# Turning the softmax weights of a first attention by VectorE and DMA instead of TensorE

## The chip, the core and the metric

The kernel runs on one core of a Trainium2 chip. The core has five engines with queues of their own: TensorE (PE, with PEld for its weight loads) does matrix products, VectorE (DVE) and ScalarE (ACT) do elementwise work, GpSimd (POOL) does next to nothing here, and SyncE (SP) issues nearly all DMAs. Each engine works off its instructions in the order in which the program was written, and waits where an instruction needs what another engine has not yet made. The metric is the device time in microseconds of one execution, the median of the runs shown.

## The reference

A decoder trunk of two layers on 256 tokens of width 2048, all in float32. Layer one uses the first attention, "mixer A"; layer two uses a second kind of attention; both have a squared-ReLU MLP and a gated embedding. The change lies in mixer A. For each of 8 heads there are three groups of keys, with dilations 1, 4 and 16:

```
for g, (window, dil) in enumerate(((128, 1), (512, 4), (2048, 16))):
    s   = q[g] . k[g] over the keys t, t - dil, t - 2 dil, ...   (window // dil + 1 of them)
    lse = logsumexp(s);  out_g = exp(s - lse) . v[g]
o = sum over g of softmax over g of (lse) * out_g
h = h + o @ w_out
```

The three softmaxes and the softmax over their `lse` are one softmax over all keys of the three groups together, and the kernel computes it so.

## The kernel before, in words

**Layout.** Activations lie feature-major: 128 features on the partitions, 256 tokens along the row. Each float32 weight chunk of 128 x 1024 (512 KB) is split into a high part `whi` (fp32r, ScalarE, L213) and a low part `wlo` (VectorE, L221), and each product is done as a sum over the parts. In mixer A the tokens stand in another order: first those with t mod 4 equal to 0 or 1, then the others. With dilations 4 and 16 a query then meets only keys of its own half, so the two halves `j` = 0, 1 of 128 queries need all 256 keys in the first group (the "far" products) and 128 keys in each of the other two (the "near" ones). So a head has 2 halves x (256 + 128 + 128) = 2 x 512 scores per query partition: the tile `p`, 128 x 2 x 512.

**The order of work.** `Program` holds a list of steps. Most are chunks: a weight chunk and a function that issues its matmuls. `run` does the following for every chunk, by step number: it issues loads of later weight chunks on SP (up to 7 ahead, 4 raw buffers), then the high-part copies (4 ahead) and the low-part subtractions (3 ahead), then `advance`, which takes every running generator to its next `yield`, and then the chunk's matmuls. An operation given by `prog.op` is begun between two chunks, and its first part, up to its first `yield`, is issued there. So a `yield` in a helper means "one chunk later", and the order of instructions on every engine follows from this list alone.

**Mixer A.** `v_unit` computes values (8 chunks each); for each head h six columns (`single`, i = 0 to 5; three q and three k, two chunks each) are computed, so that a head has 12 chunks, here numbered 0 to 11. The attention of head h - 1 runs among the columns of head h:

- after chunk 2, `a_scores(h - 1)`: 6 products of q and k (L827), then in the next three steps the masked maximum (VectorE, L834), the exponential (ScalarE, L838) and the scaling by 1/sum (VectorE, L841 and L843). The tile `p` then has queries on the partitions.
- after chunk 6, `a_transpose(h - 1)`: eight products with the identity (L852, 128x128 each) turn `p`, so that keys are on the partitions; a step later ScalarE copies the result out of PSUM (L858 the high part of the first group's blocks into `pt`, L859 the other groups' into `pl`), and another step later VectorE makes the low part (L861).
- after chunk 9, `a_pv(h - 1)`: the products with the values (L872 for the first group in three parts, L878 for the near groups in plain float32), then ScalarE and VectorE split the result into `oT` (L883, L885).

The attention of heads 6 and 7 ends later: head 6's `a_pv` and all that remains of head 7's come with `v_unit(5)` and the output projection. `twos` names chunks in which the products are issued in pairs, first two with the high part, then two with the low part; among others those which follow an inserted attention step. PSUM is used in two rings: `mm` (four banks) and `at` (two pairs of banks).

Of the kernel before, what the change touches and what calls it, by code (L numbers as in the profile page):

```python
# [10 lines left out]
F32 = mybir.dt.float32  # L11
F32R = mybir.dt.float32r
# [3 lines left out]
P = 128  # L16
D = 2048
T = 256
# [6 lines left out]
HA = 8  # L25
# [8 lines left out]
UNIT_AHEAD = (0, 1, 2, 4, 5)  # L34
# [7 lines left out]
def f32(ap):  # L42
    return ap.bitcast(F32)


def halved(ap):


    return ap.rearrange("p (h a s) -> p a h s", h=2, s=2)


def plain(ap):

    return ap.rearrange("p (a h s) -> p a h s", h=2, s=2)
# [90 lines left out]
def kernel(ctx: ExitStack, tc: tile.TileContext, a: dict, out: bass.AP):  # L145
    nc = tc.nc
    ctx.enter_context(tc.manual_schedule())
    prog = Program()
# [4 lines left out]
    tmp = ctx.enter_context(tc.tile_pool(name="tmp", bufs=2))  # L153
    xap = ctx.enter_context(tc.tile_pool(name="xa", bufs=KT))
    wpool = ctx.enter_context(tc.tile_pool(name="w", bufs=4))
    pspool = ctx.enter_context(tc.tile_pool(name="ps", bufs=1, space=bass.MemoryType.PSUM))

    cur = {}
# [9 lines left out]

    def bank():
        return pspool.tile([P, 512], F32, tag="mm", name="mm", bufs=4)  # L170

    def banks2():
        return pspool.tile([P, 2, 512], F32, tag="at", name="at", bufs=2)
# [20 lines left out]
    def load_x(j, order="xTA"):  # L194
        nc.sync.dma_start(xp[j], a[order][:, j * 2 * T:(j + 1) * 2 * T])
# [201 lines left out]
    def single(src, acts, done, mid=(), ring=bank, twos=()):  # L397

        st = []
        for c in range(2):  # L400
            def step(hi, lo, c=c):
                if c == 0:
                    st.append(ring())
                tiles = []
                for i in range(8):
                    k = 8 * c + i
                    tiles.append((st[0], i * P, have(acts, k), k == 0, k == KT - 1))
                mm_tiles(hi, lo, tiles, 2 if c in twos else 1)
                return [done(st[0])] if c else []
            prog.chunk(src(c), step)  # L410
            if c == 0:
                for fn in mid:
                    prog.op(fn)
# [361 lines left out]
    def square_pair(j):  # L775

        pa = cur["A"]
        if j == 0:
            cur["sum2"] = pa.tile([P, 2, 2 * T], F32, name="p", tag="p")[:, 0]
        total = cur["sum2"]  # L780
        s = f32(pa.tile([P, 2 * T], F32R, tag="oT", name="oT", bufs=HA)) if j else total
        nc.scalar.activation(s, xp[j], AF.Square)
        yield
        if j:
            nc.vector.tensor_add(total, total, s)
        if j == KT // 2 - 1:
            n_a0.acc = stat.tile([P, T], F32, tag="acc", name="acc")
            nc.vector.tensor_add(n_a0.acc, total[:, :T], total[:, T:])
            n_a0.done = KT

    qk, va, ready = {}, {}, {}
    oT = [None] * HA

    def qk_done(h, i, ps):
        if i == 0:
            qk[h] = cur["A"].tile([P, 6 * T], F32, tag="qk", name="qk", bufs=2)
            ready[h] = 0

        def mark():
            ready[h] += 1  # L800
        yield from to_head(ps, n_a0, qk[h][:, i * T:(i + 1) * T], True, mark)
# [15 lines left out]
    sm = {}  # L817

    def a_scores(h):

        prog.until(lambda: ready.get(h) == 6)
        sb = banks2()
        for j in range(2):
            own = slice(j * P, (j + 1) * P)
            for g in (1, 2, 0):
                q, k = qk[h][:, g * T:(g + 1) * T], qk[h][:, (3 + g) * T:(4 + g) * T]
                nc.tensor.matmul(sb[:, j, T + (g - 1) * P:T + g * P] if g else sb[:, j, :T], q[:, own],  # L827
                                 k[:, own] if g else k, start=True, stop=True)
        yield
        pa = cur["A"]  # L830
        p = pa.tile([P, 2, 2 * T], F32, tag="p", name="p")
        s4 = pa.tile([P, 4], F32, tag="s4", name="s4", bufs=2)
        for j in range(2):
            nc.vector.tensor_tensor_reduce(out=p[:, j], in0=sb[:, j], in1=cur["mA"][:, j], scale=-SCALE, scalar=3e38,  # L834
                                           op0=ALU.add, op1=ALU.min, accum_out=s4[:, j:j + 1])
        yield
        for j in range(2):
            nc.scalar.activation(p[:, j], p[:, j], AF.Exp, bias=s4[:, j:j + 1], scale=-1.0,  # L838
                                 accum_out=s4[:, 2 + j:3 + j])
        yield  # L840
        nc.vector.reciprocal(s4[:, 2:4], s4[:, 2:4])  # L841
        for j in range(2):
            nc.vector.tensor_scalar_mul(p[:, j], p[:, j], s4[:, 2 + j:3 + j])  # L843
        sm[h] = p

    def a_transpose(h):
        prog.until(lambda: h in sm)
        p = sm.pop(h)
        tr = banks2()
        for i in range(4):  # L850
            for j in range(2):
                nc.tensor.transpose(tr[:, i // 2, (i % 2 * 2 + j) * P:(i % 2 * 2 + j + 1) * P],  # L852
                                    p[:, j, i * P:(i + 1) * P], ident)
        yield
        pt = cur["A"].tile([P, 2, 2, T], F32R, tag="pt", name="pt", bufs=2)
        pl = cur["A"].tile([P, 2 * T], F32, tag="pl", name="pl", bufs=2)
        early = tr[:, 0].rearrange("p (b t) -> p b t", b=2)
        nc.scalar.copy(pt[:, :, 0, :], early)  # L858
        nc.scalar.copy(pl, tr[:, 1])  # L859
        yield  # L860
        nc.vector.tensor_sub(pt[:, :, 1, :], early, f32(pt[:, :, 0, :]))  # L861
        sm[h, "T"] = pt, pl

    def a_pv(h, wide=False):
        u0, u1 = h // 4 * 3, h // 4 * 3 + 1 + h % 4 // 2
        prog.until(lambda: (h, "T") in sm and ready.get(("v", u0)) == ready.get(("v", u1)) == 2)
        pt, pl = sm.pop((h, "T"))
        pv = (banks2()[:, 0, :] if wide else bank())[:, :T]
        c = slice(h % 4 * P, (h % 4 + 1) * P)
        def far(j):  # L870
            for vp, pp in ((0, 0), (0, 1), (1, 0)):
                nc.tensor.matmul(pv, va[u0][:, j, vp, c], pt[:, j, pp, :], start=j == vp == pp == 0,  # L872
                                 stop=j == vp == 1)
        far(0)
        for g in range(2):
            n = slice((h % 2 * 2 + g) * P, (h % 2 * 2 + g + 1) * P)
            for j in range(2):
                nc.tensor.matmul(pv[:, j * P:(j + 1) * P], va[u1][:, j, n], pl[:, g * T + j * P:g * T + (j + 1) * P],  # L878
                                 start=False, stop=False)
        far(1)  # L880
        yield
        o = cur["A"].tile([P, 2 * T], F32R, tag="oT", name="oT", bufs=HA)
        nc.scalar.copy(plain(o[:, :T]), halved(pv))  # L883
        yield
        nc.vector.tensor_sub(plain(o[:, T:]), halved(pv), plain(f32(o[:, :T])))  # L885
        oT[h] = o

    def v_unit(u, hooks=None, ring=bank, first=False):
        token_major(lambda c: a["w_v"][u * 8 + c], x_a0, lambda j, ps: v_done(u, j, ps), hooks, ring, first=first)
# [5 lines left out]
    for h in range(HA):  # L895
        for i in range(6):
            single(lambda c, h=h, i=i: a["w_qk"][(h * 6 + i) * 2 + c], x_a0,
                   lambda ps, h=h, i=i: qk_done(h, i, ps), mid=
                   [lambda h=h: a_scores(h - 1)] if h and i == 1 else
                   [lambda h=h: a_transpose(h - 1)] if h and i == 3 else  # L900
                   [lambda i=i: square_pair(2 * i)] if not h and i < 4 else (),
                   twos=(0,) if i == 0 and h in UNIT_AHEAD or i == 5 and 0 < h < HA - 1 else
                   (1,) if h and i == 1 else ())
            if not h and i < 4:
                prog.op(lambda i=i: square_pair(2 * i + 1))
            if not h and i == 3:
                prog.op(lambda: n_a0.factor(True))
            if 0 < h < HA - 1 and i == 4:
                prog.op(lambda h=h: a_pv(h - 1))
            if h in (2, 3) and i < 4:  # L910
                prog.op(lambda j=4 * h - 8 + i: load_x(j, order="xT"))
        u = (1, 2, None, 3, 4, None, None, 5)[h]
        if h == HA - 1:
            v_unit(5, {2: [lambda: a_scores(HA - 1)], 6: [lambda: a_transpose(HA - 1)],
                       7: []})
        elif u:
            v_unit(u)
# [427 lines left out]
    for h in range(HB):  # L1345
        mid = [lambda h=h: b_pv(h - 4)] if h >= 4 else []
        if h >= 3:
            mid.append(lambda h=h: b_transpose(h - 3))
        single(lambda c, h=h: a["w_q"][2 * h + c], x_a1, lambda ps, h=h: q_done(h, ps), mid,
               twos=(0, 1))  # L1350
# [127 lines left out]
```

## Time and profile before

| | |
|---|---|
| median of 3 runs | 2501.91 us (2501.83 to 2502.07) |
| profiled execution, its own time | 2502.39 us |
| its span, first to last instruction | 2500.6 us |
| mean granted TensorE clock | 0.999 |
| TensorE busy | 2489.7 us, 13405 matmuls |
| VectorE busy | 1655.1 us |
| ScalarE busy | 1346.8 us |
| moved by DMA | 468.47 MB, mean 187 GB/s |
| products with the identity in mixer A (L852) | 64, first at 105.5 us, last at 432.6 us |

How to read the views that follow. A table of groups has a line of the code, the engine, the operation, the tile written and those read (`at<-ident,p`: written to a tile named `at`, read from `ident` and `p`), shapes and a count. A row in order of time has the start in us, the length in us, engine, line, operation, names, shapes, and how many equal ones are merged; in brackets stands how long the engine was idle before it and what ended that. Records of matmuls overlap, because the array is pipelined and the recorded ends are modelled: what a matmul costs TensorE is the distance from its start to the next start. A row of landings has the number of DMAs, KB each, and the median time from issue to landing.

### The profile page before, as it was taken

To read this page: it belongs to the slowest core of one execution; us is meant where nothing else is said; L and a number is where in the kernel's file an instruction comes from. 1 tells how busy PE (TensorE), PEld (TensorE's weight loads), DVE (VectorE), ACT (ScalarE), POOL (GpSimd) and SP (SyncE) were. 2 spreads that over 40 slices of the span, in tenths; PEclk is the share of its full clock that TensorE was granted. 3 is DMA by queue.
4 is the path that set the end of the run, shared out by engine and by line. 5 is a ranking of instruction groups with operands and counts; after the bars stand their busy time and mean duration, and the time that the engine had idled before them with its cause. 6 is when DMAs were issued, how large, how long until landed. Compare 5 with 4: busy or idle time off the path is not lost.

```text
span 2500.6 us, 35900 instructions
## 1 busy us (share of the span) xinstructions
PE 2489.7 (100%) x13405; PEld 2144.8 (86%) x13405; DVE 1655.1 (66%) x2804; ACT 1346.8 (54%) x2162; POOL 10.4 (0%) x24
## 2 busy tenths in 40 slices
PE   9999999999999999999999999999999999999998
PEld 8888888888888888888888889988888888888887
DVE  7766676865465565566787989876546556556676
ACT  6444444554454453555664788755545445445455
POOL 0000000000000000000000000000000000000000
PEclk9999999999999999999999999999999999999999
DMA  8565555555656556656565744455555665665553
GB/s 274 176 199 190 175 169 181 180 190 190 192 193 193 189 191 194 192 189 187 187 196 188 245 160 124 146 191 188 193 193 191 191 192 192 193 191 190 185 187 130
DMA packets 131071, 468.47 MB, mean 187 GB/s; under 512 B 14736, under 2 KB 15696, under 8 KB 130896
## 3 DMA queue, kind: packets, MB, share of 16 engines
q1 hardware_dynamic: 129792, 464.31, 57.7%
q8 instruction: 105, 1.72, 0.3%
q0 software_dynamic: 528, 1.07, 0.1%
q10 hardware_dynamic: 576, 0.79, 0.1%
q14 instruction: 70, 0.57, 0.1%
HBM read 464.02 MB, written 2.10 MB: 186 GB/s over the span
## 4 chain that ended last, share of the span: by engine, by line
PE 97%; DMA 1%; DVE 1%; ACT 1%; issue 0%; SPq 0%; ACTq 0%; DVEq 0%
PE mm L352 22%; PE mm L442 18%; PE at L352 17%; PE at L442 15%; PE mm L354 11%; PE at L354 8%; DMA raw<-in_w_kv 1%; PE at L827 1%; PE at L1313 0%; DVE wlo L221 0%; PE mm L1337 0%; PE at L852 0%; PE mm L584 0%; PE mm L586 0%; PE mm L585 0%
## 5 line engine op out<-in xcount | busy, mean ns | idle before, releaser
L221 DVE TENSOR_TENSOR wlo<-raw,whi 128x1024 fp32r<-128x1024 f32 (+1 forms) x875 | 1065.6, 1219 | 632.4 <-PE at L442 131.8
L213 ACT CAST whi<-raw 128x1024 fp32r<-128x1024 f32 (+1 forms) x875 | 919.5, 1052 | 879.2 <-PE mm L442 200.0
L352 PE MATMUL mm<-xa,whi 128*128 128x512 f32 x2208 | 756.2, 395 | 0.0
L354 PE MATMUL mm<-xa,wlo 128*128 128x256 f32 x2208 | 575.2, 278 | 0.0
L352 PE MATMUL at<-xa,whi 128*128 128x512 f32 x1632 | 568.3, 394 | 0.0
L352 PEld LDWEIGHTS mm<-xa,whi 128*128 128x128 f32 x2208 | 399.2, 188 | 75.8 <-issue 0.4
L354 PE MATMUL at<-xa,wlo 128*128 128x256 f32 x1632 | 452.7, 277 | 0.0
L354 PEld LDWEIGHTS mm<-xa,wlo 128*128 128x128 f32 x2208 | 414.8, 188 | 20.4
L352 PEld LDWEIGHTS at<-xa,whi 128*128 128x128 f32 x1632 | 306.0, 187 | 70.4
L442 PE MATMUL at<-whi,h 128*128 128x512 f32 x1024 | 315.6, 389 | 0.0
L442 PE MATMUL mm<-whi,h 128*128 128x512 f32 x1024 | 315.5, 389 | 0.0
L354 PEld LDWEIGHTS at<-xa,wlo 128*128 128x128 f32 x1632 | 306.6, 188 | 0.1
L442 PEld LDWEIGHTS at<-whi,h 128*128 128x128 f32 x1024 | 191.9, 188 | 39.7
L442 PEld LDWEIGHTS mm<-whi,h 128*128 128x128 f32 x1024 | 191.5, 188 | 39.5
L442 PE MATMUL mm<-wlo,h 128*128 128x512 f32 x512 | 199.2, 389 | 0.0
L442 PE MATMUL at<-wlo,h 128*128 128x512 f32 x512 | 199.2, 389 | 0.0
L442 PEld LDWEIGHTS mm<-wlo,h 128*128 128x128 f32 x512 | 96.1, 188 | 20.0
L442 PEld LDWEIGHTS at<-wlo,h 128*128 128x128 f32 x512 | 96.1, 188 | 19.9
L360 DVE TENSOR_TENSOR et<-mm,es 128x256 f32<-128x256 f32 x137 | 55.9, 422 | 75.8 <-ACT es L358 73.9
L442 PE MATMUL mm<-whi,xa 128*128 128x512 f32 x320 | 98.9, 390 | 0.0
L358 ACT COPY es<-mm 128x256 f32<-128x256 f32 x137 | 48.4, 372 | 62.8 <-PE mm L354 59.9
L442 PEld LDWEIGHTS mm<-whi,xa 128*128 128x128 f32 x320 | 59.6, 188 | 12.3
(326 smaller groups left out, 2138.3 us busy)
## 6 DMA issues: line engine op xcount, KB each, us to landing
raw<-in_w SPq DMA_DIRECT2D x512, 512.0 KB, 3.5
raw<-in_w_qk SPq DMA_DIRECT2D x96, 512.0 KB, 3.6
raw<-in_w_gate SPq DMA_DIRECT2D x64, 512.0 KB, 4.0
raw<-in_w_kv SPq DMA_DIRECT2D x48, 512.0 KB, 4.2
raw<-in_w_v SPq DMA_DIRECT2D x47, 512.0 KB, 3.6
raw<-in_w_q SPq DMA_DIRECT2D x32, 512.0 KB, 4.5
raw<-in_w_oB SPq DMA_DIRECT2D x32, 512.0 KB, 3.5
raw<-in_w_oA SPq DMA_DIRECT2D x16, 512.0 KB, 3.5
```

The lines of the kernel that those rows point to most:

```text
L213: nc.scalar.copy(hi[:, c], t[:, c])
L221: nc.vector.tensor_sub(lo[:, c], t[:, c], f32(hi)[:, c])
L352: nc.tensor.matmul(ps, hi[:, col:col + P], rhs, start=first, stop=False)
L354: nc.tensor.matmul(ps[:, :T], lo[:, col:col + P], rhs[:, :T], start=False, stop=last)
L358: nc.scalar.copy(s, ps[:, :T])
L360: nc.vector.tensor_add(t, ps[:, T:], s)
L442: nc.tensor.matmul(st[j], *parts[j][i], start=k == i == 0, stop=k == kt - 1 and i == 2)
L827: nc.tensor.matmul(sb[:, j, T + (g - 1) * P:T + g * P] if g else sb[:, j, :T], q[:, own], k[:, own] if g else k, start=True, stop=True)
```

## The change

For heads 0 to 6 `a_transpose` is no longer called. Instead `a_scores` goes on into a new helper, `a_turn`, in the step of the scaling:

- step 5: VectorE's block transpose turns each 32x32 block of `p` (128 x 1024) in place of the block and writes it to a tile `z`, in an order in which the four blocks that belong to one group of 32 key partitions lie together (256 elements);
- step 6: SP stores `z` to a scratch tensor `dA` in DRAM (512 KB);
- step 7: SP loads it back in four DMAs of 32 partitions each to a tile `w`, so that the four partition groups of `dA` become four pieces of one row; a run in DRAM has 256 elements, 1 KB;
- step 9: ScalarE copies the first group's blocks to the high part of `pt`, putting pieces in order (two copies of 128 x 256);
- step 10: VectorE subtracts to make the low part (two of 128 x 256). The near groups' blocks stay in `w`; the products read them there, as four runs of 32 elements, 256 elements apart.

`a_pv(h - 1)` for heads 0 to 5 moves from after chunk 9 to after chunk 10 (the middle of column 5), and `twos` for column 5 moves from its first chunk to its second. Head 7 keeps `a_transpose`; its `pt` now takes a buffer of the ring `qk`, and its `pl` that of `z`. In the pool of mixer A two `pt` and two `pl` buffers (12 KB of a partition) are replaced by one `pt`, one `z` and one `w` (12 KB).

```diff
+    dpool = ctx.enter_context(tc.tile_pool(name="bounce", bufs=1, space=bass.MemoryType.DRAM))
...
+    def bounce(src, name, to):
+        m = src.shape[1] // 4
+        d = dpool.tile([P, 4 * m], F32, tag=name, name=name, bufs=2)
+        nc.sync.dma_start(d, src)
+        yield
+        d4 = d.rearrange("(a s) (b n) -> b s a n", a=4, b=4)
+        for b in range(4):
+            nc.sync.dma_start(to[32 * b:32 * b + 32], d4[b])
...
-        sm[h] = p
+        if h == HA - 1:
+            sm[h] = p
+            return
+        yield from a_turn(h, p)
+
+    def a_turn(h, p):
+        pa = cur["A"]
+        z = pa.tile([P, 4 * T], F32, tag="z", name="zA", bufs=1)
+        nc.vector.transpose(z.rearrange("p (b i j r) -> p j i b r", b=4, i=4, j=2), p.rearrange("p j (i b s) -> p j i b s", i=4, b=4))
+        yield
+        w = pa.tile([P, 4, T], F32, tag="w", name="wA", bufs=1)
+        yield from bounce(z, "dA", w)
+        yield
+        yield
+        pt = pa.tile([P, 2, 2, T], F32R, tag="pt", name="pt", bufs=1)
+        w5 = w.rearrange("p a (i j r) -> p i j a r", i=4, j=2)
+        pt6 = pt.rearrange("p i l (j a r) -> p l i j a r", j=2, a=4)
+        for i in range(2):
+            nc.scalar.copy(pt6[:, 0, i], w5[:, i])
+        yield
+        for i in range(2):
+            nc.vector.tensor_sub(pt6[:, 1, i], w5[:, i], f32(pt6[:, 0, i]))
+        sm[h, "T"] = pt, [[w5[:, 2 + g, j] for j in range(2)] for g in range(2)]
...
-        pt = cur["A"].tile([P, 2, 2, T], F32R, tag="pt", name="pt", bufs=2)
-        pl = cur["A"].tile([P, 2 * T], F32, tag="pl", name="pl", bufs=2)
+        pt = cur["A"].tile([P, 6 * T], F32R, tag="qk", name="pt", bufs=2)[:, :4 * T]
+        pt = pt.rearrange("p (i l t) -> p i l t", i=2, l=2)
+        pl = cur["A"].tile([P, 4 * T], F32, tag="z", name="zA", bufs=1)[:, :2 * T]
...
-                nc.tensor.matmul(pv[:, j * P:(j + 1) * P], va[u1][:, j, n], pl[:, g * T + j * P:g * T + (j + 1) * P],
+                nc.tensor.matmul(pv[:, j * P:(j + 1) * P], va[u1][:, j, n], pl[g][j],
                                  start=False, stop=False)
...
                    [lambda h=h: a_scores(h - 1)] if h and i == 1 else
-                   [lambda h=h: a_transpose(h - 1)] if h and i == 3 else
+                   [lambda h=h: a_pv(h - 1)] if 0 < h < HA - 1 and i == 5 else
                    [lambda i=i: square_pair(2 * i)] if not h and i < 4 else (),
-                   twos=(0,) if i == 0 and h in UNIT_AHEAD or i == 5 and 0 < h < HA - 1 else
-                   (1,) if h and i == 1 else ())
+                   twos=(0,) if i == 0 and h in UNIT_AHEAD else (1,) if h and i == 1 or 0 < h < HA - 1 and i == 5 else ())
...
-            if 0 < h < HA - 1 and i == 4:
-                prog.op(lambda h=h: a_pv(h - 1))
```

More of the change, by code (lines that the diff above doesn't have):

```diff
@@ L861, in a_transpose @@
         nc.vector.tensor_sub(pt[:, :, 1, :], early, f32(pt[:, :, 0, :]))
-        sm[h, "T"] = pt, pl
+        sm[h, "T"] = pt, [[pl[:, g * T + j * P:g * T + (j + 1) * P] for j in range(2)] for g in range(2)]
     def a_pv(h, wide=False):
```

## The prediction

> **What bounds the kernel now.** I read the page's busy times, the slices and the chain first: which engine is full, is it full everywhere, and does the end hang on it.
>
> ```profile
> span 2500.6 us, 35900 instructions
> PE 2489.7 (100%) x13405; PEld 2144.8 (86%) x13405; DVE 1655.1 (66%) x2804; ACT 1346.8 (54%) x2162; POOL 10.4 (0%) x24
> PE   9999999999999999999999999999999999999998
> PEclk9999999999999999999999999999999999999999
> PE 97%; DMA 1%; DVE 1%; ACT 1%; issue 0%; SPq 0%; ACTq 0%; DVEq 0%
> ```
>
> TensorE is busy in every slice at the full granted clock, and 97% of the chain that ended last is TensorE. So TensorE's instruction stream is the time: what leaves it is gained, as long as nothing makes it wait. Next, a table of one stretch in the first attention (head 3's columns, with head 2's attention among them; columns: TensorE, its weight loads, VectorE, ScalarE, GpSimd, clock, DMA share, GB/s) and the waits of the SP queue there.
>
> ```profile
> 147.00:185.00 38.00, 38.00 (x230) 33.63 (x229) 27.85 (x58) 17.30 (x26) 0.00 (x0) 1.00 0.60 193
> ```
> ```profile
> SPq L201 <- DVE wlo L221: 234.1, 92, 9.4
> ```
>
> In these 38 us TensorE has no idle time; VectorE has 10.15 us free, ScalarE 20.70, the DMA engines 40%. SP spent 234.1 us of the 270 us from 60 to 330 waiting for VectorE to free raw weight buffers, so it has time to issue more.
>
> Now TensorE's order of time at the products with the identity (L852), for the first, one middle and the last of the seven heads concerned (columns: start, length, instruction).
>
> ```profile
> 105.54 1.04 PE L852 MATMUL at<-ident,p 128*128 128x128 f32 x8
> 106.33 0.47 PE L352 MATMUL mm<-xa,whi 128*128 128x512 f32 x1
> 106.65 0.27 PE L354 MATMUL mm<-xa,wlo 128*128 128x256 f32 x1
> ```
> ```profile
> 163.03 0.28 PE L354 MATMUL mm<-xa,wlo 128*128 128x256 f32 x1
> ...
> 164.53 0.39 PE L352 MATMUL mm<-xa,whi 128*128 128x512 f32 x1
> 164.76 0.28 PE L354 MATMUL mm<-xa,wlo 128*128 128x256 f32 x1
> 164.88 1.04 PE L852 MATMUL at<-ident,p 128*128 128x128 f32 x8
> 165.67 0.47 PE L352 MATMUL mm<-xa,whi 128*128 128x512 f32 x1
> 165.99 0.27 PE L354 MATMUL mm<-xa,wlo 128*128 128x256 f32 x1
> ```
> ```profile
> 396.26 1.04 PE L852 MATMUL at<-ident,p 128*128 128x128 f32 x8
> 397.05 0.47 PE L352 MATMUL mm<-xa,whi 128*128 128x512 f32 x1
> 397.37 0.27 PE L354 MATMUL mm<-xa,wlo 128*128 128x256 f32 x1
> ```
>
> Records overlap, so starts count, not lengths. From the first product to the L354 that follows the next L352 it is 1.11 us in all three heads; without products, an L352 and its L354 start 164.76 − 164.53 = 0.23 apart. The eight products therefore cost 1.11 − 0.23 = 0.88 us a head. The L354 at 163.03 and the one five pairs on, at 164.76, give 0.346 us a pair and 8 × 0.346 = 2.77 us for a chunk of a `single`, the step in which everything is scheduled.
>
> **The change part by part.**
>
> *Products removed.* 7 heads (0 to 6; head 7 keeps them) × 0.88 = 6.16 us, all on TensorE, all on the path. The record lengths speak otherwise:
>
> ```profile
> L852 PE MATMUL at<-ident,p x64: 270/273/273, 105.5 to 432.6; 128*128 128x128 f32 x64
> ```
>
> Taken singly, 273 ns × 56 would be 15.3 us; the starts above exclude that, since eight records lie within 0.88 us. The Trainium skill (TensorE: Matmul & The Clock Gate, Part 4: PE-mode transpose) says a transpose took about 275 ns in one kernel's context, and 56 of those would be an estimated 15.4 us. The record length here agrees with it; the start to start time, which is what TensorE gives back, doesn't.
>
> *The products with v (`a_pv`) moved* from between columns 4 and 5 to the middle of column 5, and the pairwise order of the next chunk (`twos`) moved with it. Same instructions, same neighbours in kind; 0 us. But the softmax weights of the two near groups, the streamed operand of L878, are now read as four runs of 32 elements, 256 elements apart, instead of 128 in a row. I found no row with such a read. Before, this block was
>
> ```profile
> 174.07 0.52 PE L872 MATMUL mm<-pt,v 128*128 128x256 f32 x3
> 174.43 1.05 PE L878 MATMUL mm<-pl,v 128*128 128x128 f32 x8
> 175.24 0.60 PE L872 MATMUL mm<-pt,v 128*128 128x256 f32 x3
> 175.68 0.62 PE L352 MATMUL mm<-xa,whi 128*128 128x512 f32 x2
> ```
>
> where the eight records of L878 take 175.24 − 174.43 = 0.81 us. Bounds: 0, or the double, +0.81 × 7 = 5.7 us. A gain is excluded, since the same 128 columns stream. I take 0, since the same form in a row is the nearest row there is, and keep 5.7 for the range.
>
> *VectorE.* Added per head: one transpose of 128x1024 and two subtractions of 128x256; removed: one subtraction of 128x512 (0.69 in the rows below). The transpose is new; the nearest row of its size is the weight subtraction, 1.21; the shuffle, the nearest by kind, 0.43 per 256 elements, would make it 1.72. I take 1.21, since size sets it in these rows (0.42 at 256 columns, 0.69 at 512). Sum +1.21 + 2 × 0.42 − 0.69 = +1.36 (or +1.87) a head, against 10.15 us free: 0 on the path. Were VectorE full, it would be 7 × 1.36 = 9.5 us.
>
> ```profile
> 158.82 0.88 DVE L843 TENSOR_SCALAR p<-p,s 128x512 f32<-128x512 f32 x2
> ...
> 159.63 0.43 DVE L463 STREAM_SHUFFLE rsh<-et 32x256 f32<-32x256 f32 x1
> ...
> 167.07 0.69 DVE L861 TENSOR_TENSOR pt<-at,pt 128x512 fp32r<-128x512 f32 x1 [0.23 <-ACT pl L859]
> 169.13 0.42 DVE L360 TENSOR_TENSOR et<-mm,es 128x256 f32<-128x256 f32 x1 [1.37 <-ACT es L358]
> ...
> 172.06 1.21 DVE L221 TENSOR_TENSOR wlo<-raw,whi 128x1024 fp32r<-128x1024 f32 x1
> ```
>
> *ScalarE.* Two copies of 128x512 from PSUM go (0.59 + 0.60), two of 128x256 from SBUF come; the copy of that size quoted below, to `oT`, took 0.37. About −0.4 a head; off the path, since ScalarE is free for more than half of the stretch.
>
> *SP and the DMA queue.* Five DMAs a head, 512 KB out and 4 × 128 KB back. Two rows for SP's time, and the landings:
>
> ```profile
> raw<-in_w_qk SPq DMA_DIRECT2D x96, 512.0 KB, 3.6
> out<-h SPq DMA_DIRECT2D x5, 256.0 KB, 2.0
> ps<-in_pT POOLq DMA_DIRECT2D x4, 128.0 KB, 2.9
> ```
> ```profile
> L201 SPq DMA_DIRECT2D raw<-in_w_qk x96: 327/328/346, 17.9 to 387.8; - x96
> DMA to landing us min/median/max: 3.3/3.6/7.3
> ```
> ```profile
> 164.32 17.07 SPq L201 DMA_DIRECT2D raw<-in_w_qk  x6
> 181.44 0.43 SPq L195 DMA_DIRECT2D x<-in_xT  x1
> ```
>
> An issue costs 0.33 to 0.43 us: 1.65 to 2.15 a head. The new waits are on SP: the write waits for the transpose, the reads for the write's landing, and weight loads queue behind. Head 2's chain, with chunks numbered 0 to 11 within head 3: scaling ends 158.82 + 0.88 = 159.70, the transpose, next on VectorE, 160.9; write issued in step 6, landing (no row for a store of this size; 2.0 for half of it, 3.6 for a load of 512 KB in the same traffic, 7.3 at the worst; I take 3.6) at 164.5; four reads issued by 165.8, the last landing at 169.4 with 3.6 again (2.9 is the lower row). Meanwhile the load of step 8, which went out at 164.32 before, goes at about 166: 2 us late. By the code, VectorE splits in step s the weight chunk that TensorE uses in step s + 3: the subtraction at 172.06 is step 10's and ends some 11 us before TensorE reaches its chunk at about 184 (175.68 + 3 × 2.77). So 2 us late at SP hides behind that lead; if the lead were gone it would be 2 × 7 = 14 us.
>
> *Does the turned tile arrive in time?* The products with v are now due when chunk 10 ends: 174.07 − 0.88 + 2.77 = 175.96. Before them ScalarE copies (step 9, 2 × 0.37 = 0.74) and VectorE subtracts (step 10, 0.84). The data must have landed by 175.96 − 1.58 = 174.4; I expect 169.4. Margin 5 us, so 0 us on the path. The legs may take 13.5 us where I count 8.5. ScalarE stands idle meanwhile, as it did before without harm:
>
> ```profile
> 175.88 0.37 ACT L883 CAST oT<-mm 128x256 fp32r<-128x256 f32 x1 [3.40 <-PE mm L872]
> ```
>
> For head 6 the products are in the output projection, far later.
>
> *Traffic and buffers.* 1 MB more per head of some 37 us is +28 GB/s on 193, 40% free: 0. The tiles swap one for one (12 KB before, 12 after): 0.
>
> *Sum.* −6.16 + 0 = −6.16 us. The profiled execution took 2502.39 (span 2500.6 plus 1.79 around it), 0.48 above the median of the runs, 2501.91; −6.16 on the median gives 2495.75, on the profiled one 2496.2. I say 2495.8.
>
> **The rivals.** 0.2% of this time, about what its measurement can tell, is 5.0 us: below 2496.9 is faster, above 2506.9 slower.
>
> - *A, forecast:* 2495.8, own range 2495.0 to 2496.8.
> - *B, the trip through DRAM comes late*, at the first product with v of heads 0 to 5. With the worst landing row for both legs: 160.9 + 7.3 = 168.2, last read issued 1.3 later, landed 176.8, copies and subtractions done 178.4, against 175.96: 2.4 us a head, six heads, +14.6, that is 2510.4. It cancels the gain at 1.03 us a head (legs of 14.5 us) and is slower from 1.86. For it: a store to DRAM and its wait appear nowhere in this stage, and the reads come in rows of 1 KB. Against it: 5 us of margin, and the 7.3 belongs to one of 96 loads. The Trainium skill has a rule that speaks for it (VectorE: DVE Perf Modes, The three transpose paths): a plain DMA copy that transposes by strides is 19 times slower than the crossbar. By that an estimated 19 × 3.6 = 68 us would go into the read alone, and the time would pass 2800; its condition, a large innermost stride, isn't met by rows of 256 elements in sequence, and no run here shows it. I give this extreme 0.01 of B's chance.
> - *C, strided reads cost TensorE*: L878 doubles, −6.16 + 5.7, 2501.4, no change. Nothing speaks for it but the missing row.
> - *D, the gain was hidden*: TensorE is held by the split weights, and the freed 0.88 us turn into waiting; 2501.9. Against it: no idle time of TensorE in the stretch above and a lead of 11 us.
> - *E, small change:* waits of 0.2 to 0.5 us a head where a product with v now waits for two engines and four DMAs: 2497 to 2499.5, no change.
>
> **How the numbers follow.** A 0.72, B 0.11 (0.10 of it slower, 0.01 within), C 0.06, D 0.05, E 0.06. Faster 0.72, same 0.18, slower 0.10. The range reaches from 2494.6 (1.2 us more gain than counted) through C, D and E to 2502.6; B is left out, and 0.03 below and in between.
>
> **What would show it.** No L852 before head 7; the eight that stay at about 432. The L354 of each chunk 7 then follows at the usual 0.23. A new VectorE group of 128x1024 ×7 near 1.2 us. Seven stores landing near 3.6 us and 28 reads. L878 to the next L872 still 0.81 apart. TensorE idle before L872: nothing; a ScalarE wait for the read DMAs at the new copies may show and cost nothing. Wrong if TensorE waits before L872 (B, E), if L878 widens (C), or if L352 waits for ScalarE's `whi` (D).

## The result, and the profile after

Ten runs each, on the same chip: 2495.53 us (2495.07 to 2495.74) after, 2502.02 us (2501.83 to 2502.17) before. The ratio is 0.9974, 95% interval 0.9966 to 0.9982. The change gained 6.49 us where 6.16 were forecast; 2495.8 was the predicted time, and 2495.53 is below 2496.9, the prediction's bound for faster. The profiled execution took 2495.55.

The page of the kernel after, its span, busy times and chain:

```profile
span 2493.8 us, 35888 instructions
PE 2482.9 (100%) x13349; PEld 2138.5 (86%) x13349; DVE 1663.7 (67%) x2818; ACT 1345.3 (54%) x2162; POOL 10.4 (0%) x24
PE 99%; DMA 0%; ACT 0%; issue 0%; DVE 0%; SPq 0%; ACTq 0%; DVEq 0%
```

TensorE has 56 matmuls fewer (13405 to 13349, 7 heads x 8 products), is 6.8 us less busy, and is as full as before. (Line numbers are 14 higher up to `a_scores`, then more: L366 and L368 are L352 and L354 of before, L841 is L827, L910 and L916 are L872 and L878.)

A correction of names first: the stretch from 147 us on, which the prediction and the expectations call head 2's attention among head 3's columns, is head 1's attention among head 2's columns (the first scores, at 92.67, are head 0's). No number hangs on it. TensorE's order of time after, where the products with the identity stood in that stretch (the join of chunks 6 and 7), and then the products with v:

```profile
163.54 0.39 PE L366 MATMUL mm<-xa,whi 128*128 128x512 f32 x1
163.77 0.27 PE L368 MATMUL mm<-xa,wlo 128*128 128x256 f32 x1
163.88 0.40 PE L366 MATMUL mm<-xa,whi 128*128 128x512 f32 x1
164.11 0.28 PE L368 MATMUL mm<-xa,wlo 128*128 128x256 f32 x1
```
```profile
174.86 0.27 PE L368 MATMUL mm<-xa,wlo 128*128 128x256 f32 x1
174.97 0.51 PE L910 MATMUL mm<-pt,v 128*128 128x256 f32 x3
175.32 1.05 PE L916 MATMUL mm<-wA,v 128*128 128x128 f32 x8
176.13 0.60 PE L910 MATMUL mm<-pt,v 128*128 128x256 f32 x3
```

The join is gapless: 0.11 from an L368 to the next L366, 0.23 to the next L368. The products with v start 0.11 after the L368 in front of them, so they waited for nothing; L916, which now reads four runs of 32, takes 176.13 − 175.32 = 0.81 us, as before.

The gain can be read head by head. The first two and the last scores of the eight heads, before and after:

```profile
92.67 1.92 PE L827 MATMUL at<-qk 128*128 128x128 f32 x12
152.01 1.92 PE L827 MATMUL at<-qk 128*128 128x128 f32 x12
...
419.19 1.04 PE L827 MATMUL at<-qk 128*128 128x128 f32 x6
```
```profile
92.58 1.92 PE L841 MATMUL at<-qk 128*128 128x128 f32 x12
151.01 1.92 PE L841 MATMUL at<-qk 128*128 128x128 f32 x12
...
412.76 1.92 PE L841 MATMUL at<-qk 128*128 128x128 f32 x12
```

Between the first row and the last lie seven heads and everything that was removed: 326.52 us before, 320.18 after, 6.34 less, 0.906 a head. The other 0.15 us of the gain lies outside the first attention, where two runs of one program differ by as much: the changed kernel, run again (`after_again` below), shows the same 320.18 between these marks and a median 0.25 us lower. Head 1's scores, 151.01 for 152.01, are 1.0 us earlier, so times of this stretch after are to be read as about one later on the clock of before.

The turn itself, of head 1's weights. SP's queue, VectorE and ScalarE of the kernel after:

```profile
160.02 0.33 SPq L180 DMA_DIRECT2D dA<-zA  x1
162.61 0.33 SPq L215 DMA_DIRECT2D raw<-in_w_qk  x1
163.54 2.28 SPq L184 DMA_DIRECT2D wA<-dA  x4
165.86 0.43 SPq L209 DMA_DIRECT2D x<-in_xT  x1
166.40 12.89 SPq L215 DMA_DIRECT2D raw<-in_w_qk  x6
```
```profile
158.75 1.25 DVE L867 STREAM_TRANSPOSE zA<-p 128x1024 f32<-128x1024 f32 x1
...
170.19 1.20 DVE L235 TENSOR_TENSOR wlo<-raw,whi 128x1024 fp32r<-128x1024 f32 x1
171.32 0.74 DVE L880 TENSOR_TENSOR pt<-wA,pt 128x256 fp32r<-128x256 f32 x2
```
```profile
169.30 0.71 ACT L877 CAST pt<-wA 128x256 fp32r<-128x256 f32 x2 [1.13 <-DMA wA<-dA]
173.45 1.05 ACT L227 CAST whi<-raw 128x1024 fp32r<-128x1024 f32 x1 [3.44 <-DMA raw<-in_w_qk]
```

The store goes out at 160.02, the loads follow from 163.54, and ScalarE, which had waited 1.13 us for them, starts to copy at 169.30; VectorE is done at 172.06, 2.9 us before the products begin. The median landings of the two legs (the store, and each of the four loads):

```profile
dA<-zA SPq DMA_DIRECT2D x7, 512.0 KB, 3.5
wA<-dA SPq DMA_DIRECT2D x28, 128.0 KB, 4.0
```

The second ScalarE row shows what the trip costs others. The weight load that SP issued at 166.40, behind the four loads, landed 7.0 us later; its row:

```profile
L215 SPq DMA_DIRECT2D raw<-in_w_qk x1: 365/365/365, 166.4 to 166.4; - x1
DMA to landing us min/median/max: 7.0/7.0/7.0
```

ScalarE waited 3.44 us for it, and none of that reached TensorE, which comes to this chunk, the third behind chunk 11, only at about 185 (176.57 and three chunks of 2.77 us). The table of the stretch that stood in the prediction, now one us shorter:

```profile
147.00:184.00 37.00, 37.00 (x222) 32.68 (x221) 28.95 (x59) 16.67 (x25) 0.00 (x0) 1.00 0.69 226
```

VectorE is at 28.95 of 37 us (27.85 of 38 before), the DMA engines at 0.69 (0.60), TensorE without a gap.

### The profile page after: what moved, and what is told of

Its sections match the earlier page's. It is cut to its first block, busy times and chain, and to the rows that moved or that the text cites. A ratio compares the mean times of both kernels' runs of the same rounds, so it can differ in the third digit from the quotient of the medians.

```text
span 2493.8 us, 35888 instructions
## 1 busy us (share of the span) xinstructions
PE 2482.9 (100%) x13349; PEld 2138.5 (86%) x13349; DVE 1663.7 (67%) x2818; ACT 1345.3 (54%) x2162; POOL 10.4 (0%) x24
## 4 chain that ended last, share of the span: by engine, by line
PE 99%; DMA 0%; ACT 0%; issue 0%; DVE 0%; SPq 0%; ACTq 0%; DVEq 0%
PE mm L366 23%; PE mm L456 18%; PE at L366 17%; PE at L456 17%; PE mm L368 11%; PE at L368 8%; PE at L841 1%; PE at L1348 0%; PE mm L1372 0%; PE mm L1104 0%; PE mm L1105 0%; PE mm L598 0%; PE mm L600 0%; PE mm L599 0%; PE at L1298 0%; DMA raw<-in_w_v 0%
## 5 line engine op out<-in xcount | busy, mean ns | idle before, releaser
L366 PE MATMUL mm<-xa,whi 128*128 128x512 f32 x2208 | 755.2, 395 | 0.0
L368 PE MATMUL mm<-xa,wlo 128*128 128x256 f32 x2208 | 575.4, 278 | 0.0
L366 PE MATMUL at<-xa,whi 128*128 128x512 f32 x1632 | 568.3, 394 | 0.0
L366 PEld LDWEIGHTS mm<-xa,whi 128*128 128x128 f32 x2208 | 399.3, 188 | 76.1 <-issue 0.4
L368 PE MATMUL at<-xa,wlo 128*128 128x256 f32 x1632 | 453.1, 278 | 0.0
L368 PEld LDWEIGHTS mm<-xa,wlo 128*128 128x128 f32 x2208 | 414.9, 188 | 20.3
L366 PEld LDWEIGHTS at<-xa,whi 128*128 128x128 f32 x1632 | 306.1, 188 | 70.3
L368 PEld LDWEIGHTS at<-xa,wlo 128*128 128x128 f32 x1632 | 306.7, 188 | 0.1
L372 ACT COPY es<-mm 128x256 f32<-128x256 f32 x137 | 48.4, 371 | 68.8 <-PE mm L368 65.8
```

Of the source, the lines that this page charges most:

```text
L366: nc.tensor.matmul(ps, hi[:, col:col + P], rhs, start=first, stop=False)
L368: nc.tensor.matmul(ps[:, :T], lo[:, col:col + P], rhs[:, :T], start=False, stop=last)
L372: nc.scalar.copy(s, ps[:, :T])
```

## The experiments

**What a product with the identity costs** (`twice`). The kernel before, the products issued twice for heads 0 to 6:

```diff
-        for i in range(4):
+        for i in list(range(4)) * (2 if h < HA - 1 else 1):
             for j in range(2):
                 nc.tensor.transpose(tr[:, i // 2, ...], p[:, j, i * P:(i + 1) * P], ident)
```

> The kernel before, with the eight products with the identity issued twice for heads 0 to 6 (the second eight write the same values to the same place). Theory A (TensorE's stream is the time, and a product costs the distance between starts, not its record): eight more products cost 0.79 us by the starts of the trace before (from the first product to the next L352), without the 0.09 of the first pair behind them; 7 x 0.79 = 5.5, so 2507.5 us, and not above 2508.2 (7 x 0.88). Rival D (such products lie in time that TensorE would wait anyway): 2502.0. Rival of the record length (273 ns each): 7 x 8 x 0.273 = 15.3, 2517.3.

Measured: 2508.46 us against 2502.08, ratio 1.0025 (1.0015 to 1.0035). That is +6.38, 0.91 a head. Between the marks used above, the first and the last scores, its trace shows 332.64 us against 326.52: 6.12 more, 0.874 a head; the other 0.26 lies outside the first attention. Its TensorE in order of time, at the same place:

```profile
165.57 0.28 PE L354 MATMUL mm<-xa,wlo 128*128 128x256 f32 x1
165.69 1.91 PE L852 MATMUL at<-ident,p 128*128 128x128 f32 x16
167.35 0.47 PE L352 MATMUL mm<-xa,whi 128*128 128x512 f32 x1
167.67 0.27 PE L354 MATMUL mm<-xa,wlo 128*128 128x256 f32 x1
```

Sixteen take 1.66 us where eight took 0.79, so the second eight cost 0.87. The expectation of 5.5 was too small, because it took the first eight's 0.79, whose cost reaches into the pair behind them (the 0.09 that the prediction had counted). The stated limit, 2508.2, fits the 6.12 of the trace; the median passed it by 0.26. The reading of D falls: TensorE has no idle time there into which products could go. So does the record length of 273 ns, which asked for 15.3.

**Whether the trip costs anything** (`no_turn`). The changed kernel without transpose, store and loads:

```diff
-        z = pa.tile([P, 4 * T], F32, tag="z", name="zA", bufs=1)
-        nc.vector.transpose(z.rearrange(...), p.rearrange(...))
         yield
         w = pa.tile([P, 4, T], F32, tag="w", name="wA", bufs=1)
-        yield from bounce(z, "dA", w)
+        nc.vector.tensor_copy(w.rearrange("p a t -> p (a t)"), p.rearrange("p j t -> p (j t)"))
+        yield
         yield
         yield
```

> The changed kernel without the block transpose and without the trip through DRAM: VectorE copies the softmax weights as they are into the tile w, one copy of 128x1024 in the step of the store, and all that follows is as in the changed kernel. What is left out: the softmax weights are not turned, so the attention output is not the reference's. Theory A (the trip is wholly hidden): the time of the changed kernel, 2495.5, within 0.3. Rival (the trip costs TensorE something by waits or by late weights): below 2495.2 by what it costs.

Measured: 2495.72 us, ratio to before 0.9975 (0.9965 to 0.9984); the changed kernel had 0.9974. Without the trip nothing is gained: it is wholly hidden. (VectorE still makes one pass over the tile here, the copy, 0.68 us for 1.25; whether it has room for the transpose is what `dve4` below asks.)

**Whether the move of the products with v did something** (`moved`). The kernel before with this alone:

```diff
+                   [lambda h=h: a_pv(h - 1)] if 0 < h < HA - 1 and i == 5 else
...
-            if 0 < h < HA - 1 and i == 4:
-                prog.op(lambda h=h: a_pv(h - 1))
```

(and `twos` as in the change.)

> The kernel before with the products with v of heads 0 to 5 and the pairwise chunk moved as in the change, and nothing else: the products with the identity stay. Theory A: 2502.0, within 0.2. Rival (the move gives the 0.3 us by which the change gained more than 6.16): 2501.7.

Measured: 2502.14 us against 2502.08, ratio 1.0 (0.9991 to 1.0009). Its trace has the same 326.52 us between the first and the last scores as before. The move is worth nothing, so the 0.3 us above the forecast aren't its doing.

**Whether four runs of 32 cost TensorE something** (`row`). The changed kernel with the near groups' weights put in a row first, for heads 0 to 5:

```diff
...
+        pl = z[:, :2 * T]
+        pl6 = pl.rearrange("p (i j a r) -> p i j a r", i=2, j=2, a=4)
+        for i in range(2):
+            nc.scalar.copy(pl6[:, i], w5[:, 2 + i])
...
```

> The changed kernel with ScalarE copying the near groups' weights of heads 0 to 5 into 128 columns in a row (two copies of 128x256 into z, in the step of the subtractions) before TensorE reads them. Theory A (reading four runs of 32 costs TensorE nothing): 2495.5, within 0.3. Rival C (it costs something that the starts don't show): below 2495.2.

Measured: 2495.25 us, beside the changed kernel run again on the same chip (`after_again`):

> The changed kernel again, beside the two others on the same chip: 2495.5, within 0.3, under every theory. It is the base for the tenths.

which gave 2495.28 (both ratios to before have the interval 0.9963 to 0.9984). C falls, by these medians and by the 0.81 us of L916 above: the strided read costs TensorE nothing that shows.

**How much time the trip has** (four runs). Two put the products with v earlier, one makes the trip longer, one delays its start. They ran on another chip than the rest, where the kernel before took 2501.87 us; the changed kernel was not run there, so they are set against its 2495.53, and tenths are not to be read.

`early1` and `early2`, the changed kernel with the products after chunk 9 and after chunk 8, and one or two steps less between loads and copies:

```diff
         yield from bounce(z, "dA", w)
         yield
-        yield
...
-                   [lambda h=h: a_pv(h - 1)] if 0 < h < HA - 1 and i == 5 else
+            if 0 < h < HA - 1 and i == 4:
+                prog.op(lambda h=h: a_pv(h - 1))
```

```diff
         yield from bounce(z, "dA", w)
-        yield
-        yield
...
-                   [lambda h=h: a_pv(h - 1)] if 0 < h < HA - 1 and i == 5 else
+                   [lambda h=h: a_pv(h - 1)] if 0 < h < HA - 1 and i == 4 else
```

(`twos` follows in both.)

> The changed kernel with the products with v of heads 0 to 5 one chunk earlier, where they were before the change, and one step less between the loads and the copies. In the changed kernel's trace head 2's tile has landed at 169.3, VectorE is done at 172.1, and the products start at 175.0. One chunk earlier they are due at 172.2; without the wait for its step VectorE is done at about 170.9. Theory A (what counts is landing plus 1.6 us against the due time): no wait, 2495.5, within 0.5. Rival B (the trip is at its limit already): 2499 or more.

> The same two chunks earlier: the products are due at 169.4, the tile lands at 169.3, copies and subtractions need 1.6 more, so TensorE waits about 1.5 us at each of six heads. Theory A: 2495.5 + 9 = 2504.5, between 2501 and 2510. Rival (something else than the landing sets the wait, or there is cover that the trace doesn't show): 2495.5.

Measured: `early1` 2497.11 us (2496.28 to 2498.60), ratio 0.9981 (0.9972 to 0.9991); `early2` 2501.33 (2499.88 to 2503.95), ratio 0.9998 (0.9989 to 1.0008). TensorE of `early2` in order of time, at head 1:

```profile
169.79 0.27 PE L368 MATMUL mm<-xa,wlo 128*128 128x256 f32 x1
171.69 0.96 PE L908 MATMUL mm<-pt,v 128*128 128x256 f32 x3 [1.63 <-ACT pt L875]
```

The wait stands where rival B put it, ahead of the products with v, released by the copy that waited for the loads. One chunk (2.77 us) earlier the margin is gone at head 1; two chunks earlier the gain of the change is. The size for `early2` was over-estimated: 5.8 us more than the changed kernel, not 9, because the head from which I had worked it out, head 1, is the slowest: the weight loads of L908 waited 1.94 us there and 0.30 to 0.62 at the five others, and a further 0.27 or so for VectorE each. `early1` lost 1.6 us where I had expected none. Its profiled execution, its fastest, is 1.25 us longer than the changed kernel's between the first and the last scores (321.43 for 320.18). VectorE and then TensorE of `early1` at head 1:

```profile
170.29 0.42 DVE L374 TENSOR_TENSOR et<-mm,es 128x256 f32<-128x256 f32 x1 [4.12 <-ACT es L372]
```
```profile
172.23 0.51 PE L909 MATMUL mm<-pt,v 128*128 128x256 f32 x2 [0.22 <-DVE pt L879]
```

From the first product with v to L915, which follows the first three, it is 0.85 us at head 1 (171.73 to 172.58) and 0.53 at head 3, against 0.35 in the changed kernel, so 0.50 and 0.18 were lost there. The tile wasn't what came late at head 1: ScalarE began to copy it at 169.27. But with one step less, this copy, which waited 4.40 us for the loads, stands in ScalarE's queue ahead of the copy `es` (L372), and VectorE waited 4.12 us for `es` and then had a weight subtraction to do before it came to the tile at 171.76. This is read from the trace; no run tests it. Most of the rest of the 1.25 us is slower pairs behind the wait, told of in the last section. The wider spread of both kernels' runs is what a wait for DMA would give; the longer executions were not profiled.

`long_trip`, one more store and load ahead of the turning trip, and `dve4`, the block transpose four times:

```diff
+        d0 = dpool.tile([P, 4 * T], F32, tag="d0", name="d0", bufs=2)
+        nc.sync.dma_start(d0, z)
+        yield
+        nc.sync.dma_start(z, d0)
         yield from bounce(z, "dA", w)
         yield
-        yield
```

```diff
-        nc.vector.transpose(z.rearrange(...), p.rearrange(...))
+        for _ in range(4):
+            nc.vector.transpose(z.rearrange(...), p.rearrange(...))
```

> The changed kernel with one more trip through DRAM (z stored, loaded back to z) ahead of the one that turns; the steps of copies and products stay. Two more legs of 3.5 us: the tile lands at about 169.3 + 7 = 176.3, VectorE is done at 177.9, the products are due at 175.0: 2.9 us for six heads. Theory A: 2495.5 + 17 = 2513, between 2505 and 2520; the trip becomes the bound, and the wait stands ahead of the products with v. Rival (SP's queue is what breaks: loads behind the waits come late and the ordinary products wait for whi): the same or more time, but the wait stands ahead of the products with the weights. Rival (more cover than counted): 2495.5.

> The changed kernel with the block transpose issued four times in a row: 3 x 1.25 = 3.7 us more on VectorE a head, which had 8 us free in 37, and the store starts 3.7 us later. Theory A: landing 173.0, VectorE done at 174.6 to 175.4, products due at 175.0: between no wait and 0.9 us for six heads, 2495.5 to 2500.6. Rival (VectorE's cover is gone: split weights come late everywhere): 2495.5 + 7 x 3.7 = 2521 at the most.

Measured: `long_trip` 2515.32 us, ratio 1.0058 (1.0042 to 1.0075); `dve4` 2495.46, ratio 0.9975 (0.9965 to 0.9984). In `dve4` the subtractions and the products meet, in head 1 (VectorE, then TensorE):

```profile
174.63 0.74 DVE L881 TENSOR_TENSOR pt<-wA,pt 128x256 fp32r<-128x256 f32 x2
```
```profile
175.14 0.51 PE L911 MATMUL mm<-pt,v 128*128 128x256 f32 x3
```

The store of `dve4` went out 4.0 us later (164.03 for 160.02; 3.8 later if the scores are laid upon each other, 151.18 for 151.01), the subtractions end at 175.37, and the products wait for nothing: by the code the first three read only the half that the first of the two subtractions makes, and that one, 0.41 us long, ends at about 175.04. So a start of the store that is 3.8 us later still fits, barely, and VectorE had the room for 26 us of useless transposes (7 x 3 x 1.25). In `long_trip` it is used up, and the waits at the products with v (rows of the view of waits on TensorE's weight loads, in all, times, longest):

```profile
PEld mm L913 <- ACT pt L880: 14.0, 6, 4.6
PEld mm L913 <- DVE pt L883: 1.5, 6, 0.3
```

These are 15.5 us, but the kernel lost 19.8 against the changed one. The rest is mostly the clock, told of in the last section.

**Head 7 too** (`head7`, `head7b`). If the theory holds, eight more products can go. `head7` turns the last head in the same way; its chain is short, since the output projection needs it:

```diff
-        if h == HA - 1:
-            sm[h] = p
-            return
         yield from a_turn(h, p)
...
+        last = h == HA - 1
         yield from bounce(z, "dA", w)
         yield
-        yield
+        if not last:
+            yield
```

(its `w` and `pt` take buffers of the ring `qk`, and the call of `a_transpose` goes.)

> The changed kernel with head 7 turned in the same way too, one step less between the loads and the copies, its w and pt in the ring qk. Theory A: eight more products go, 0.88 us, 2494.6, if the tile is there when the second chunk of the output projection ends; by the steps it has 10 us for the two legs from about 420 and needs about 8.5. Rival (it comes late): above 2495.5 by the wait, 1 us or more.

Measured: 2496.10 us, ratio to before 0.9976 (0.9967 to 0.9985): 0.57 us above the changed kernel, not 0.9 below. ScalarE and TensorE show why:

```profile
429.23 0.71 ACT L877 CAST pt<-wA 128x256 fp32r<-128x256 f32 x2 [3.03 <-DMA wA<-dA]
429.84 1.26 ACT L825 ACTIVATE v<-mm,col 128x512 f32<-128x512 f32 x2
```
```profile
430.57 0.73 PE L366 MATMUL mm<-oT,whi 128*128 128x512 f32 x2 [1.19 <-ACT v L825]
```

ScalarE stood 3.03 us at the copy that waits for the loads, and behind it in the same step stood the copies of the last values out of PSUM. The output projection's next products needed their banks: from the L368 at 429.00 to the L366 at 430.57 it is 1.57 us, where 0.23 is usual. So nobody was yet in need of the copy that waited; what did harm is that others stood behind it. `head7b` issues the turned tile's copies of head 7 behind the chunk's matmuls, and so behind those:

```diff
-        if not last:
-            yield
+        yield "tensor" if last else None
```

> As the run head7 (head 7 turned too), but ScalarE's copies of the turned tile of head 7 are issued behind the chunk's matmuls and so behind the two copies of the last values (v, L825), which in head7 stood behind them and made the output projection wait 1.4 us for its banks. Theory A with this reading: the wait goes, the gain of head 7's products stays, 2494.6, and TensorE shows no wait at the output projection. Rival (head 7's products were not worth 0.88 there, or the copies come too late for the products with v): 2495.5 or more.

Measured: 2494.61 us, ratio to before 0.9971 (0.9960 to 0.9983), beside 2495.28 for the changed kernel on the same chip: 0.67 less, where 0.88 was expected; medians of one program differ by 0.25 here. Its ScalarE:

```profile
427.50 1.37 ACT L825 ACTIVATE v<-mm,col 128x512 f32<-128x512 f32 x2 [1.17 <-PE mm L456]
429.20 0.71 ACT L876 CAST pt<-wA 128x256 fp32r<-128x256 f32 x2 [0.33 <-DMA wA<-dA]
```

The values leave first, the tile lands at the same moment, and no wait of TensorE is left in the first attention. It is the fastest version here.

## Why the prediction was right, point by point

- *Products removed, 6.16.* Right, in kind and nearly in size: 6.49 in the medians, 6.34 between the marks of the two traces. The term of 0.88 a head measured 0.906 when the products were taken out and 0.874 when they were issued again (`twice`, between the same marks; the 6.38 of its medians has 0.26 from outside this stage). Taking starts instead of record lengths was the step that mattered. What the 0.03 a head is I can't say; the move isn't it (`moved`).
- *Products with v moved, four runs of 32: 0.* Right: 0.81 us for L916 as before, and `moved` and `row` within 0.1 us of their bases.
- *VectorE +1.36 a head, hidden.* Right: the transpose took 1.25 (1.21 taken, 1.72 the upper end), and `dve4` shows that three more had room.
- *SP and the landings.* The store was counted at 3.6 and landed in 3.5. The tile was expected at 169.4 on the clock of before; ScalarE began on it at 169.30, which is 170.3 on that clock, 0.9 later, since the four issues took 2.28 us instead of 1.3 to 1.7. The load behind them went out at 166.40, or 167.4, for 164.32: 3.1 us late where 2 were forecast. Then it took 7.0 us to land instead of 3.6, which the prediction hadn't at all. The lead of the split weights covered it.
- *Margin 5 us.* Too large: in the trace VectorE ends 2.9 us before the products begin, since the tile came 0.9 later than counted and VectorE then had a weight subtraction (1.20) to end first. The runs give no single figure. `dve4`, with the store 3.8 us later, loses nothing; `early1`, with the reader 2.77 us earlier, loses 1.6, because it changes the order in the queues too, which the count from landing to reader leaves out.
- *Rivals.* B is a true mechanism that this placing stays clear of: `early2` and `long_trip` bring it about, with the wait exactly at the products with v. The rule of the Trainium skill that the prediction weighed beside it (VectorE: DVE Perf Modes, The three transpose paths: 19 times slower by strides) did not show with runs of 1 KB: the loads back, 128 KB each, landed in 4.0 us, near the 3.6 of the plain weight loads of 512 KB. C falls by `row`, D by `twice`, E by the gapless rows at 174.86 and 174.97 and by the view of waits, which has none for TensorE or its weight loads from 30 to 480 us. E's upper end was mis-added: 0.5 us at six heads gives 2498.8, not 2499.5.

## What to carry to other kernels

Where one engine's stream is the time, price a removed instruction by the distance between starts, and then ask of the substitute only whether it arrives in time: count from the last producer to the first reader, and test it by moving the reader a step earlier. In a queue that works in order, an instruction that waits is harmless only if what stands behind it can wait as well, so put the waiting ones last in their step. A round trip through DRAM for half a megabyte took 8.9 to 9.7 us here, from the issue of the store to the copy that waited for the loads (seven heads of the changed kernel), and a load issued behind it landed in 7.0 us instead of 3.6.

## What I had not expected of the hardware

**TensorE's clock falls after a long wait.** `long_trip` lost 4.3 us more than its waits (19.8 against 15.5). The table of its stretches around its two longest waits, at the products with v of heads 1 (3.5 us, until 179.3) and 2 (4.6 us, until 223.0) (the columns as in the prediction, the clock third from the right):

```profile
179.00:183.00 4.00, 3.60 (x16) 3.23 (x17) 2.93 (x8) 3.34 (x7) 0.00 (x0) 0.68 0.65 259
183.00:187.00 4.00, 4.00 (x22) 3.51 (x21) 2.93 (x7) 1.79 (x3) 0.00 (x0) 0.89 0.67 190
...
215.00:219.00 4.00, 3.72 (x22) 2.96 (x20) 0.00 (x0) 0.00 (x0) 0.00 (x0) 1.00 0.91 248
219.00:223.00 4.00, 0.00 (x0) 0.00 (x0) 0.00 (x0) 0.43 (x2) 0.00 (x0) 0.80 0.94 350
223.00:227.00 4.00, 3.97 (x16) 3.71 (x17) 3.23 (x8) 2.78 (x6) 0.00 (x0) 0.50 0.11 46
227.00:231.00 4.00, 4.00 (x21) 3.40 (x20) 2.29 (x5) 1.72 (x4) 0.00 (x0) 0.84 0.73 236
```

After 4.6 us without work the granted clock is 0.50 for the next four microseconds and 0.84 for the four after them, after 3.5 us 0.68 and 0.89. That is (0.50 + 0.16 + 0.32 + 0.11) x 4 = 4.4 us of lost clock, about the 4.3 that the waits leave open. In windows of one microsecond the clock is 0.50 from about 180.5 to 183.9, so it fell 1.2 us after work had begun again, and from about 221.6, still in the wait, to 228.1. The kernel's mean clock is 0.997, against 0.999 for the others. `early2`, whose longest wait is 1.94 us, keeps 0.999. The Trainium skill (TensorE: Matmul & The Clock Gate, Part 1: The HAM clock gate) states an idle window of about 3.4 us after which the clock halves until about as long a stretch of work. The traces agree on the halving, with 1.94 us below the window and 3.5 and 4.6 above. The half clock lasted 3.4 us at head 1, but 5.1 us of work at head 2.

**Pairs can run slower behind a wait, at the full clock.** In `early1` the L366 from 176.61 to 187.56 are 0.353 us apart, and so are those from 192.47 to 209.08, at a granted clock of 1.00; before the wait at head 1 and in all of the changed kernel's first attention it is 0.347. Over these 78 pairs that is 0.5 us. The same 0.353 stands behind waits in `early2` and `long_trip` (185.73 to 193.86 and on to 218.20, after the clock is back at 1.00), and in `early1` it is gone behind head 2's products with v. What causes it stays open.

**An issue on SP can take four times its usual time.** The four loads back, in `after` and in `early1` (shortest, median and longest issue in ns):

```profile
L184 SPq DMA_DIRECT2D wA<-dA x28: 325/424/852, 104.5 to 393.2; - x28
```
```profile
L184 SPq DMA_DIRECT2D wA<-dA x28: 325/424/1672, 104.1 to 392.5; - x28
```

The issue of 852 ns lies in the four at 163.54. The DMA engines are at 0.73 in the 2.4 us of these issues and at 0.98 in the 3.4 us behind them; whether a full DMA queue is the cause wasn't tested.

```profile
163.50:165.90 2.40, 2.40 (x16) 2.10 (x15) 2.37 (x7) 1.05 (x1) 0.00 (x0) 1.00 0.73 263
165.90:169.30 3.40, 3.40 (x21) 2.98 (x20) 2.77 (x6) 1.32 (x3) 0.00 (x0) 1.00 0.98 230
```
